# A recurrence decode that loads its next state block while it works, and weight casts issued three groups ahead

## The chip, the core and the metric

The kernel runs on one core of a Trainium2 chip. Its five engines work side by side, each through its own instruction queue in order: TensorE (PE; its weight loads are PEld), VectorE (DVE), ScalarE (ACT), GpSimd (POOL) and SyncE (SP), which issues all transfers here. The metric is the device time of one launch in microseconds (us).

## What is computed

One inference step of a two-layer decoder trunk. A prompt of 256 tokens and 8 decode tokens (one for each of 8 sequences) share all weights. Each layer has eight retention heads and sixteen heads of the RWKV-7 recurrence side by side, an output projection, and a gated feed-forward block of width 5632:

```python
xn   = rms_norm(h, g_attn);  proj = xn @ w_in            # 2048 -> 7456 columns
y_ret, s_ret = retention_mixer(proj[:, :4096], ret_state, ...)
y_rw,  s_rw  = rwkv7_mixer(shifted(proj[:, 4096:]), rwkv_state, ...)
h = h + concat(y_ret, y_rw) @ w_out
hn = rms_norm(h, g_ffn)
h = h + (silu(hn @ w_gate) * (hn @ w_up)) @ w_down

def step(s, inp):                      # the recurrence, for one token
    sa = einsum('bhvk,bhk->bhv', s, -kk)
    s  = s * w + sa[..., None] * (kk * a) + v[..., None] * k
    return s, einsum('bhvk,bhk->bhv', s, r)
```

For the 8 decode tokens the recurrence is one such step on a stored state of 128 x 64 x 64 numbers for each layer (8 sequences x 16 heads on the partitions).

## The kernel before, in words

**Weights.** All weights are packed into one stream of 128x128 blocks. `Stream` loads eight blocks at a time (`w_raw`, 512 KB, four buffers), rounds four at a time to fp32r on ACT (`w_hi`), and subtracts on DVE to get the rounding error (`w_lo`). Each block feeds three matmuls into the PSUM tile `st`: `w_hi` times the rounded activations, `w_hi` times their error, `w_lo` times the rounded activations. `proj` runs sixteen blocks for one output block; `contract` runs the blocks of the output projection and of `w_down`. The 19,872 `st` matmuls stand in a fixed order: per layer 59 projections for attention, the output projection in three phases (`W_OUT`: heads 0 to 3 of retention; recurrence pairs 0 to 3 with head 4; the rest), then the feed-forward block in four quarters.

**Side work.** Everything else is a set of generators. After every block `tick` lets each of them issue its next few instructions in the order of `RANK` (smaller first), by a small model of the engines' clocks, `Clock`; when PE has nothing to issue (`need`, `take`) only the side work goes on. So a fixed program comes out: each engine has its own order, and a matmul that needs a late tile holds up all matmuls behind it.

**The recurrence.** The sixteen heads go in eight pairs. `g_pair` prepares a pair; `g_levels` and `g_seq` (rank 2 and 1) run its chain over four chunks of 64 tokens: `py` on PE, its negative into `c_rT` (one half by DVE, one by ACT), then PE, ACT (`Z1`), PE, DVE (`r`), PE, ACT (`Z`), PE, DVE (`S`). Three buffers of the ring TM (8, shared with the tiles `h` of the residual stream) are held until a chain ends. `g_out` (rank 3) turns it into a block for the output projection.

**Its decode.** `g_rwkv_decode` (rank 4.5) starts when all pairs have given up their decode columns. It reads the state in eight blocks `dS` of 256 KB. For each block POOL multiplies it by one vector into `dT`, DVE sums that (`dec_sa`), DVE multiplies the block by another vector into a second `dT` and sums that (`dec_o`). `dS` and `dT` share two buffers (tag `d3`). At the end there is a norm, a transpose on PE (`o2`) and the tile `dec_y`, which POOL puts into the blocks of the output projection; phase 1 of `W_OUT` waits for it. `g_ret_state` (rank 5) does the like for the retention heads with `rkb`, `rS`, `rqb` in three buffers (tag `d2`); `g_update` (rank 6) writes the new recurrence state during the feed-forward block.

Of the kernel before, what the change touches and what calls it, by code (L numbers as in the profile page):

```python
# [19 lines left out]
P = 128  # L20
# [19 lines left out]
RC = 8  # L40
RAW_BUFS = 4
CH = 4
HL_BUFS = 4
CAP = {"st": 3, "pw": 5, "qa": 2, "qb": 2, "qc": 2, "gy": 3, "blk": 27, "TM": 8, "y": 1}
TA, RR, LV, UB, US, U2 = 4, 3, 2, 5, 5, 4
NORM_EPS = 1e-6
RET_EPS = 1e-5
RWKV_EPS = 64e-5
# [135 lines left out]


class Stream:
    def __init__(self, nc, clock, pools, src, ahead):
        self.nc, self.clock, self.pools, self.src = nc, clock, pools, src
        self.n = src.shape[0] * RC // CH
        self.raw, self.hi, self.lo = {}, {}, {}  # L190
        self.loaded = self.made = self.split = self.pos = 0
        self.ahead = ahead

    def load(self):
# [6 lines left out]
        r, i = divmod(c, RC // CH)  # L201
        return self.raw[r][:, i * CH:(i + 1) * CH]

    def make(self):
        r = self.made // (RC // CH)
        while self.loaded < min(self.src.shape[0], r + RAW_BUFS):
            self.load()
        h = self.hi[self.made] = self.pools[1].tile([P, CH, P], F32R, name="w_hi")
        self.nc.scalar.activation(out=h, in_=self.part(self.made), func=AF.Copy)
        self.made += 1  # L210

    def make_lo(self):
        c = self.split
        l = self.lo[c] = self.pools[2].tile([P, CH, P], F32R, name="w_lo")
        eng = self.nc.gpsimd if c < KB // CH else self.nc.vector
        eng.tensor_tensor(out=l, in0=self.part(c), in1=self.hi[c].bitcast(F32), op=ALU.subtract)
        self.split += 1

    def next(self):
        c, i = divmod(self.pos, CH)  # L220
        while self.made < min(self.n, c + 1 + self.ahead):
            self.make()
        while self.split < self.made and (self.split <= c + 1 or
                                          self.clock.at(self.hi[self.split]) <= self.clock.now + 100):
            self.make_lo()
        self.pos += 1
        return self.hi[c][:, i], self.lo[c][:, i]


EARLY = 150  # L230
GATE = 600
RANK = {"seq": 1, "levels": 2, "solve": 2, "pair": 3, "out": 3, "ret": 4, "rout": 4, "dec": 4.5, "state": 5, "upd": 6}


class Task:
# [7 lines left out]
class Kern:  # L243
# [4 lines left out]
    def __init__(self, ctx, tc, a, o):  # L248
        self.clock = Clock()
        self.tc, self.nc, self.a, self.o, self.ctx = tc, Core(tc.nc, self.clock), a, o, ctx  # L250
        nc = self.nc

        def pool(name, bufs=1, **kw):
            return Pool(ctx.enter_context(tc.tile_pool(name=name, bufs=bufs, **kw)), name, bufs, self.clock)

        self.const = pool("const")
        self.blk = pool("blk", bufs=CAP["blk"])
        self.st = pool("st", bufs=CAP["st"], space=PSUM)
        self.pw = pool("pw", space=PSUM)
# [7 lines left out]
        self.stream = Stream(nc, self.clock, (pool("w_raw", RAW_BUFS), pool("w_hi", HL_BUFS), pool("w_lo", HL_BUFS)), a["ws"],  # L267
                             HL_BUFS - 1)
# [455 lines left out]
    def g_seq(self, l, p, sv, AR, cf, LA, KA, TM, bv, Y):  # L724
# [6 lines left out]
        for c in range(NC):  # L731
# [5 lines left out]
                nc.tensor.matmul(py[:, 0:P], lhsT=ar, rhs=S, start=False, stop=True)  # L737
            yield 1
            rT = self.rT[:, c % 2]
            nc.vector.tensor_scalar(out=rT[lo, lo], in0=py[lo, lo], scalar1=-1.0, scalar2=None, op0=ALU.mult)  # L740
            nc.scalar.activation(out=rT[hi, hi], in_=py[lo, hi], func=AF.Copy, scale=-1.0)
            oc = un.tile([P, P], F32, name="oc", tag="us", bufs=US)
            nc.scalar.activation(out=oc[hi], in_=py[hi, 0:P], func=AF.Copy)
# [147 lines left out]
    def g_rwkv_decode(self, l, pds):  # L891
# [3 lines left out]
        scr = self.dr.tile([NS, NP, 2, 6, CW], F32, name="scr_dec")  # L895
        rows = 6 * NS
        for g in range(2):
            dt = de.tile([P, 4, P], F32, name="dec_t", tag="d3", bufs=2)
# [26 lines left out]
        od = de.tile([P, CW], F32, name="dec_o", bufs=1)  # L925
        sa = sm.tile([P, CW], F32, name="dec_sa", bufs=1)
        VB = 8
        for j in range(CW // VB):
            js = slice(j * VB, j * VB + VB)
            S = de.tile([P, VB, CW], F32, name="dS", tag="d3", bufs=2)  # L930
            nc.sync.dma_start(out=S, in_=self.a["s_rwkv"][l, :, js])
            yield 4
            for vec, dst in ((kr, sa), (wr, od)):
                tm = de.tile([P, VB, CW], F32, name="dT", tag="d3", bufs=2)
                eng = nc.gpsimd if vec is kr else nc.vector
                eng.tensor_tensor(out=tm, in0=S, in1=bc(vec, 1, VB), op=ALU.mult)
                yield 2
                nc.vector.tensor_reduce(out=dst[:, js], in_=tm, axis=AX.X, op=ALU.add)
                yield 4
        dd = sm.tile([P, 2], F32, name="dec_dd")  # L940
        for i, x in enumerate((kn, km)):
            t = sm.tile([P, CW], F32, name="dec_sq")
# [25 lines left out]
        for p in sorted(range(NP), key=lambda p: "b" not in self.Y[8 + p]):  # L968
# [3 lines left out]
            self.Y[8 + p]["dec"] = True  # L972
            yield 1

    def g_update(self, l):
        nc, de = self.nc, self.de
        w, v, km, sa, kn = self.upd
        VB = 8
        for j in range(CW // VB):
            js = slice(j * VB, j * VB + VB)  # L980
            S = de.tile([P, VB, CW], F32, name="uS", tag="d3", bufs=2)
            nc.sync.dma_start(out=S, in_=self.a["s_rwkv"][l, :, js])
            yield 13
# [71 lines left out]
    def g_ret_state(self, l, h, d, scr):  # L1055
# [270 lines left out]
    def layer(self, l):  # L1326
        nc = self.nc
        if l == 0:
# [301 lines left out]
```

## Time and profile before

| | us |
|---|---|
| median of 3 runs | 2911.83 (2911.44 to 2912.65) |
| the profiled execution | 2910.49 |
| its span, first to last instruction | 2908.6 |
| PE busy, weight loads busy | 2762.9 (95%), 2732.5 |
| DVE busy | 2047.8 (70%) |
| ACT busy | 1434.6 (49%) |
| POOL busy | 813.8 (28%) |

The profiled execution is 1.3 us below the median. 1.9 us of it lie outside the span. Layer 0 ends at about 1394 us; its attention and output projection take the time to about 692, and the feed-forward block the rest. The second layer has the same stages from 1394 to 2895.

### The profile page before, as it was taken

The page shows a single profiled execution, that of the slowest core. Times are in us where ns is not written, and L with a number is a line of the kernel's source. Part 1 is how long each engine was busy: PE and PEld are TensorE (multiplying, and loading weights), DVE is VectorE, ACT ScalarE, POOL GpSimd, SP SyncE. Part 2 cuts the span into 40 slices and gives each one's busy share as a digit, 9 for nine tenths or more (in the row PEclk, how much of TensorE's full clock was granted, in tenths as well). Part 3 has the DMA queues.
Part 4 walks back from the last instruction along what each step waited for, and adds up shares of the span by engine and source line. Part 5 has one row for each costly group of instructions (what it writes and reads, how often), then busy time and mean ns, then how long its engine had stood idle before and what let it go on. Part 6 is the DMA issues. An engine that isn't in the chain of part 4 may idle for free.

```text
span 2908.6 us, 58897 instructions
## 1 busy us (share of the span) xinstructions
PE 2762.9 (95%) x22304; PEld 2732.5 (94%) x22304; DVE 2047.8 (70%) x3964; ACT 1434.6 (49%) x2823; POOL 813.8 (28%) x1315
## 2 busy tenths in 40 slices
PE   7999999959999999999999999997899999999998
PEld 6998999859999999999999999996899999999998
DVE  7787777858856656666677778878688566665665
ACT  5554555425444444445555555543455454444454
POOL 4555655514500000000135655644153000000001
PEclk9999999979999999999999999998899999999999
DMA  5555555735655555555654545556466555555554
GB/s 171 158 161 162 157 161 165 234 111 191 223 182 181 181 182 181 182 181 182 204 171 131 169 154 181 166 171 212 146 201 209 181 181 182 182 181 182 181 182 138
DMA packets 230828, 512.46 MB, mean 176 GB/s; under 512 B 57488, under 2 KB 105872, under 8 KB 230544
## 3 DMA queue, kind: packets, MB, share of 16 engines
q1 hardware_dynamic: 230544, 508.70, 54.6%
q8 instruction: 175, 2.87, 0.4%
q14 instruction: 109, 0.89, 0.1%
HBM read 485.24 MB, written 23.38 MB: 175 GB/s over the span
## 4 chain that ended last, share of the span: by engine, by line
PE 81%; DVE 5%; DMA 2%; issue 1%; ACT 1%; POOL 1%; DVEq 0%; SPq 0%; POOLq 0%; ACTq 0%
PE st L161 73%; PE pw L161 7%; DVE w_lo L161 2%; DMA dS<-in_s_rwkv 1%; DVE on L161 1%; POOL dT L161 0%; DMA rkb<-scr_qk 0%; DVE dec_sa L161 0%; DVE dT L161 0%; DVE h L161 0%; ACT w_hi L161 0%; ACT rsw L161 0%; DVE blk L161 0%; DVE rS L161 0%; DVE q L161 0%
## 5 line engine op out<-in xcount | busy, mean ns | idle before, releaser
L161 PE MATMUL st<-blk,w_hi 128*128 128x264 f32 (+1 forms) x13248 | 2529.7, 290 | 27.0 <-DVE blk L161 19.4
L161 PEld LDWEIGHTS st<-blk,w_hi 128*128 128x128 f32 x13248 | 2064.4, 189 | 35.5 <-ACT w_hi L161 22.4
L161 PE MATMUL st<-blk,w_lo 128*128 128x264 f32 (+1 forms) x6624 | 1892.8, 286 | 13.1 <-DVE w_lo L161 10.2
L161 DVE TENSOR_TENSOR w_lo<-w_raw,w_hi 128x512 fp32r<-128x512 f32 x1652 | 1234.0, 752 | 595.0 <-ACT w_hi L161 564.4
L161 ACT ACTIVATE w_hi<-w_raw 128x512 fp32r<-128x512 f32 x1656 | 1043.2, 631 | 1162.4 <-PE st L161 1075.5
L161 PEld LDWEIGHTS st<-blk,w_lo 128*128 128x128 f32 x6624 | 1252.2, 189 | 17.1 <-DVE w_lo L161 12.7
L161 POOL TENSOR_TENSOR acc<-acc,sq 128x264 f32<-128x264 f32 x72 | 59.7, 829 | 1426.3 <-ACT sq L161 1425.9
L161 DVE TENSOR_TENSOR h<-h,st 128x264 f32<-128x264 f32 x224 | 94.8, 424 | 22.7 <-PE st L161 22.6
L161 POOL TENSOR_TENSOR sv_x<-sv_x,sv_t 32x15 f32<-32x15 f32 (+7 forms) x240 | 88.4, 368 | 18.8
L161 POOL TENSOR_TENSOR sv_t<-sv_m,sv_x 32x15 f32<-32x15 f32 (+7 forms) x240 | 84.1, 351 | 27.1 <-DMA sv_m<-scr_l 11.5
L161 ACT ACTIVATE c_rT<-pw 64x64 f32<-64x64 f32 x64 | 13.8, 216 | 89.1 <-DVE c_rT L161 88.8
L161 POOL TENSOR_TENSOR brs<-bve,c_nhalf 128x4 f32<-128x4 f32 (+3 forms) x42 | 41.5, 988 | 56.3 <-DVE bve L161 52.9
L161 ACT ACTIVATE Z<-pw 128x128 f32<-128x128 f32 x128 | 35.1, 274 | 41.8 <-PE pw L161 40.1
L161 POOL TENSOR_SCALAR mix_d<-mix_p,c_vec 128x8 f32<-128x8 f32 x54 | 34.7, 642 | 58.9 <-DVE mix_p L161 54.0
L161 POOL TENSOR_TENSOR Lm<-LA,c_m_lv 128x512 f32<-128x512 f32 x32 | 46.8, 1461 | 14.6 <-PE pw L161 14.5
L161 POOL TENSOR_TENSOR rqb<-rS,rqb 128x512 f32<-128x512 f32 x32 | 44.7, 1396 | 22.1 <-DMA rqb<-scr_qk 12.8
L161 POOL TENSOR_TENSOR uS<-uS,uT 128x512 f32<-128x512 f32 x32 | 48.6, 1519 | 2.5
L161 DVE TENSOR_TENSOR fg<-st,c_R 128x264 f32<-128x264 f32 x88 | 38.0, 432 | 13.7 <-PE st L161 13.0
L161 PE MATMUL pw<-c_ident,o 128*128 128x128 f32 x2 | 0.9, 447 | 48.6 <-DVE o L161 48.6
L161 DVE TENSOR_TENSOR fg<-st,fg 128x264 f32<-128x264 f32 x88 | 37.9, 431 | 12.2 <-PE st L161 12.2
L161 PEld LDWEIGHTS pw<-c_ident,o 128*128 128x128 f32 x2 | 0.4, 182 | 48.9 <-issue 48.9
L161 POOL TENSOR_TENSOR rkb<-rkb,v 128x512 f32<-128x512 f32 x32 | 35.2, 1099 | 39.4 <-DMA rkb<-scr_qk 39.4
(232 smaller groups left out, 2310.2 us busy)
## 6 DMA issues: line engine op xcount, KB each, us to landing
w_raw<-in_ws SPq DMA_DIRECT2D x828, 512.0 KB
rkb<-scr_qk SPq DMA_DIRECT2D x32, 256.0 KB
rS<-in_s_ret SPq DMA_DIRECT2D x32, 256.0 KB
rqb<-scr_qk SPq DMA_DIRECT2D x32, 256.0 KB
out_sts<-rS SPq DMA_DIRECT2D x32, 256.0 KB
h<-in_x SPq DMA_DIRECT2D x16, 264.0 KB
dS<-in_s_rwkv SPq DMA_DIRECT2D x16, 256.0 KB
uS<-in_s_rwkv SPq DMA_DIRECT2D x16, 256.0 KB
```

The costliest lines, as they stand in the source:

```text
L161: return f(*a, **kw)
```

## The change

Five things change.

1. In the decode of the recurrence `dec_load` issues the load of the next block right after POOL's product with the current one, and the second product of DVE goes into `dS` itself, so that a block has one `dT` and not two. The generator waits for the modelled end of a tile where it counted ticks before.
2. The tags `d2` (three buffers) and `d3` (two) become one ring `d` of five, used by the decode, the retention state and the state update. Rank of the decode: 4.5 to 1; of the retention state: 5 to 3.
3. `w_hi` has five buffers and not four, and is cast three groups ahead at a group's first block and four from the second; `w_lo` follows two or three groups ahead by position and no longer by the modelled end of `w_hi`. One `w_raw` tile fewer is loaded ahead, at the start too.
4. The first half of `c_rT` moves from DVE to ACT.
5. To make room, the rings `gy` (gates), `rr` and `u` lose a buffer each: 3 to 2, 3 to 2, 5 to 4.

```diff
-HL_BUFS = 4
-CAP = {"st": 3, "pw": 5, "qa": 2, "qb": 2, "qc": 2, "gy": 3, "blk": 27, "TM": 8, "y": 1}
-TA, RR, LV, UB, US, U2 = 4, 3, 2, 5, 5, 4
+HI_BUFS, LO_BUFS = 5, 4
+AHEAD = 3
+CAP = {"st": 3, "pw": 5, "qa": 2, "qb": 2, "qc": 2, "gy": 2, "blk": 27, "TM": 8, "y": 1}
+TA, RR, LV, UB, US, U2, DB = 4, 2, 2, 4, 5, 4, 5
...
-    def make(self):
-        r = self.made // (RC // CH)
-        while self.loaded < min(self.src.shape[0], r + RAW_BUFS):
-            self.load()
...
+    def make_hi(self, c):
+        while self.his <= min(c, self.n - 1):
+            r = self.his // (RC // CH)
+            while self.loaded < min(self.src.shape[0], r + RAW_BUFS - 1):
+                self.load()
+            h = self.hi[self.his] = self.pools[1].tile([P, CH, P], F32R, name="w_hi")
+            self.nc.scalar.activation(out=h, in_=self.part(self.his), func=AF.Copy)
+            self.his += 1
...
     def next(self):
         c, i = divmod(self.pos, CH)
-        while self.made < min(self.n, c + 1 + self.ahead):
-            self.make()
-        while self.split < self.made and (self.split <= c + 1 or
-                                          self.clock.at(self.hi[self.split]) <= self.clock.now + 100):
-            self.make_lo()
+        on = self.ahead > 0
+        self.make_hi(c + self.ahead + (on and i > 0))
+        self.make_lo(c + self.ahead - (on and i < 2))
...
-RANK = {"seq": 1, "levels": 2, "solve": 2, "pair": 3, "out": 3, "ret": 4, "rout": 4, "dec": 4.5, "state": 5, "upd": 6}
+RANK = {"seq": 1, "levels": 2, "solve": 2, "pair": 3, "out": 3, "ret": 4, "rout": 4, "dec": 1, "state": 3, "upd": 6}
...
-            nc.vector.tensor_scalar(out=rT[lo, lo], in0=py[lo, lo], scalar1=-1.0, scalar2=None, op0=ALU.mult)
+            nc.scalar.activation(out=rT[lo, lo], in_=py[lo, lo], func=AF.Copy, scale=-1.0)
...
+        S = self.dec_load(l, 0)
         for j in range(CW // VB):
             js = slice(j * VB, j * VB + VB)
-            S = de.tile([P, VB, CW], F32, name="dS", tag="d3", bufs=2)
-            nc.sync.dma_start(out=S, in_=self.a["s_rwkv"][l, :, js])
-            yield 4
-            for vec, dst in ((kr, sa), (wr, od)):
-                tm = de.tile([P, VB, CW], F32, name="dT", tag="d3", bufs=2)
-                eng = nc.gpsimd if vec is kr else nc.vector
-                eng.tensor_tensor(out=tm, in0=S, in1=bc(vec, 1, VB), op=ALU.mult)
-                yield 2
-                nc.vector.tensor_reduce(out=dst[:, js], in_=tm, axis=AX.X, op=ALU.add)
-                yield 4
+            yield (self.clock.at(S),)
+            tm = de.tile([P, VB, CW], F32, name="dT", tag="d", bufs=DB)
+            nc.gpsimd.tensor_tensor(out=tm, in0=S, in1=bc(kr, 1, VB), op=ALU.mult)
+            nxt = self.dec_load(l, j + 1) if j + 1 < CW // VB else None
+            yield (self.clock.at(tm),)
+            nc.vector.tensor_tensor(out=S, in0=S, in1=bc(wr, 1, VB), op=ALU.mult)
+            nc.vector.tensor_reduce(out=sa[:, js], in_=tm, axis=AX.X, op=ALU.add)
+            yield (self.clock.at(S),)
+            nc.vector.tensor_reduce(out=od[:, js], in_=S, axis=AX.X, op=ALU.add)
+            S = nxt
...
+    def dec_load(self, l, j):
+        S = self.de.tile([P, 8, CW], F32, name="dS", tag="d", bufs=DB)
+        self.nc.sync.dma_start(out=S, in_=self.a["s_rwkv"][l, :, 8 * j:8 * j + 8])
+        return S
```

What the change does to the order is seen at two places. The first is VectorE's queue in layer 0 where phase 0 of the output projection ends; `h` are its sums into the residual stream, `ret_y` the decode of the retention heads, `dec_sa` and `dec_o` the sums of the decode. Before:

```order
L161 TENSOR_SCALAR on<-pw,bmv,brs 16x128
L161 TENSOR_TENSOR h<-h,st 128x264
L161 TENSOR_TENSOR w_lo<-w_raw,w_hi 128x512
L161 TENSOR_REDUCE dec_sa<-dT 128x8
L161 TENSOR_TENSOR ret_y<-pw,rgd 128x16
L161 TENSOR_TENSOR ret_y<-ret_y,c_vec 128x16
L161 TENSOR_TENSOR h<-h,st 128x264
L161 TENSOR_TENSOR dT<-dS,dec_wr 128x512
L161 TENSOR_REDUCE dec_o<-dT 128x8
L161 TENSOR_REDUCE dec_sa<-dT 128x8
L161 TENSOR_TENSOR dT<-dS,dec_wr 128x512
```

After, VectorE's queue a little earlier in the same stretch; `r`, `S` and `o` belong to the last pair's chain, `ry` and `rS` to the retention heads:

```order
L162 TENSOR_TENSOR dS<-dS,dec_wr 128x512
L162 TENSOR_REDUCE dec_sa<-dT 128x8
L162 SCALAR_TENSOR_TENSOR ry<-pw,c_vec,rg 128x256
L162 TENSOR_REDUCE dec_o<-dS 128x8
L162 TENSOR_TENSOR r_8354<-c_rT,pw 128x128
L162 TENSOR_TENSOR dS<-dS,dec_wr 128x512
L162 TENSOR_REDUCE dec_sa<-dT 128x8
L162 SCALAR_TENSOR_TENSOR S<-pw,cf,Sc 128x128
L162 TENSOR_REDUCE dec_o<-dS 128x8
L162 TENSOR_TENSOR o<-pw,oc 64x128
L162 SCALAR_TENSOR_TENSOR rS<-rS,rkb 128x512
```

Before, the fourth of the eight blocks stands among the last sums `h` of phase 0, and four more follow with nothing between them; after, the fifth and sixth block shown here stand among the last chain's instructions, and the eighth is done before phase 0 ends. A block has three instructions on this queue both times.

The second place is SyncE's queue over the same stretch; `rkb`, `rS`, `rqb` and `out_sts` are the retention state's transfers. Before:

```order
L161 DMA w_raw<-in_ws 128x1024
L161 DMA h<-in_x 128x528
L161 DMA out_sts<-rS 128x512
L161 DMA w_raw<-in_ws 128x1024
L161 DMA dS<-in_s_rwkv 128x512
L161 DMA w_raw<-in_ws 128x1024 x2
L161 DMA dS<-in_s_rwkv 128x512 x4
L161 DMA w_raw<-in_ws 128x1024 x24
```

After:

```order
L162 DMA dS<-in_s_rwkv 128x512
L162 DMA out_sts<-rS 128x512
L162 DMA rkb<-scr_qk 128x4x128
L162 DMA dS<-in_s_rwkv 128x512
L162 DMA rS<-in_s_ret 128x512
L162 DMA dS<-in_s_rwkv 128x512
L162 DMA rqb<-scr_qk 128x4x128
L162 DMA dS<-in_s_rwkv 128x512
L162 DMA out_srp<-S 64x64 x2
L162 DMA h<-in_x 128x528
L162 DMA upg<-in_up 128x256
L162 DMA w_raw<-in_ws 128x1024
```

Before, the last four loads of `dS` follow each other behind the weights `w_raw`; after, the last four stand earlier, among the loads of the retention state, and none is left behind the weights.

## Rows read from the trace of the kernel before

**Rows 1.** Windows by stage: busy us of each engine, granted clock, DMA share, GB/s.
```profile
531.00:586.00 55.00, 47.81 (x346) 44.52 (x344) 49.54 (x120) 21.73 (x55) 26.11 (x30) 0.94 0.77 246
586.00:618.00 32.00, 1.52 (x7) 1.05 (x7) 15.08 (x36) 0.63 (x1) 7.98 (x14) 0.57 0.17 50
618.00:1394.00 776.00, 775.16 (x6373) 774.63 (x6373) 516.94 (x848) 378.90 (x650) 72.67 (x68) 1.00 0.57 185
...
1971.00:2018.00 47.00, 42.53 (x333) 40.56 (x331) 43.84 (x105) 20.07 (x47) 22.09 (x26) 1.00 0.80 259
2018.00:2046.00 28.00, 1.38 (x7) 0.64 (x5) 15.46 (x38) 0.63 (x1) 9.19 (x13) 0.55 0.17 56
2046.00:2895.00 849.00, 845.87 (x6948) 844.72 (x6948) 550.86 (x911) 419.95 (x725) 83.33 (x84) 1.00 0.56 181
```

**Rows 2.** Chain of waits, 586 to 618: start us, us, what.
```profile
588.40 2.89 DMA dS<-in_s_rwkv
...
591.42 1.27 POOL dT L161
592.71 0.70 DVE dec_sa L161
...
594.22 2.75 DMA dS<-in_s_rwkv
...
611.03 0.69 DVE dec_o L161
...
617.32 0.87 PE st L161 x2
```

**Rows 3.** Waits of VectorE, 586 to 618: us in total, times, longest.
```profile
DVE dec_sa L161 <- POOL dT L161: 14.1, 4, 3.7
```

**Rows 4.** Waits of VectorE, 2018 to 2046.
```profile
DVE dec_sa L161 <- POOL dT L161: 9.9, 4, 3.7
```

**Rows 5.** Waits of TensorE, whole span.
```profile
PE pw L161 <- DVE o L161: 48.6, 2, 28.8
...
PE pw L161 <- ACT c_rT L161: 12.2, 9, 2.8
PE st L161 <- DVE w_lo L161: 10.2, 7, 3.8
```

**Rows 6.** Tile c_rT, whole span: idle time of its engines, us and times.
```profile
  DVE c_rT L161: 88.8, 53
```

**Rows 7.** Tile c_rT, 531 to 618: duration ns min/median/max, first and last start.
```profile
L161 DVE TENSOR_SCALAR c_rT<-pw x4: 206/208/209, 534.1 to 561.6; 64x64 f32<-64x64 f32 x4
```

**Rows 8.** Groups of VectorE, 531 to 586: busy us, mean ns, idle before.
```profile
L161 DVE TENSOR_TENSOR w_lo<-w_raw,w_hi 128x512 fp32r<-128x512 f32 x21 | 17.7, 854 | 0.4 <-ACT w_hi L161 0.4
```

**Rows 9.** Groups of VectorE, 700 to 1390.
```profile
L161 DVE TENSOR_TENSOR w_lo<-w_raw,w_hi 128x512 fp32r<-128x512 f32 x474 | 347.3, 736 | 218.6 <-ACT w_hi L161 208.3
```

**Rows 10.** Timeline of VectorE, 706 to 730: start us, us, instruction.
```profile
709.50 0.43 DVE L161 TENSOR_TENSOR fg<-st,c_R 128x264 f32<-128x264 f32 x1 [0.18 <-PE st L161]
...
710.95 1.27 DVE L161 SCALAR_TENSOR_TENSOR fg<-fth,fg 128x264 f32<-128x264 f32 x1
...
718.28 0.42 DVE L161 TENSOR_TENSOR blk<-fg,blk 128x264 fp32r<-128x264 f32 x1
...
721.30 0.43 DVE L161 TENSOR_TENSOR fg<-st,c_R 128x264 f32<-128x264 f32 x1 [0.18 <-PE st L161]
...
722.45 0.42 DVE L161 SCALAR_TENSOR_TENSOR fg<-fth,fg 128x264 f32<-128x264 f32 x1
```

**Rows 11.** Windows of the st matmuls alone, after the first gap.
```profile
617.30:620.00 2.70, 2.68 (x12) 2.68 (x13) 0.00 (x0) 0.00 (x0) 0.50 0.64 191
620.00:622.00 2.00, 2.00 (x13) 2.00 (x13) 0.35 (x1) 0.00 (x0) 0.68 0.01 4
...
700.00:702.00 2.00, 2.00 (x18) 2.00 (x18) 0.00 (x0) 0.00 (x0) 1.00 0.59 219
```

**Rows 12.** Waits of SyncE's queue, 531 to 618.
```profile
SPq L161 <- DVE dT L161: 13.7, 4, 5.3
```

More of the change, by code (lines that the diff above doesn't have):

```diff
@@ L186, with __init__ @@
 class Stream:
-    def __init__(self, nc, clock, pools, src, ahead):
-        self.nc, self.clock, self.pools, self.src = nc, clock, pools, src
+    def __init__(self, nc, pools, src, ahead):
+        self.nc, self.pools, self.src = nc, pools, src
         self.n = src.shape[0] * RC // CH
         self.raw, self.hi, self.lo = {}, {}, {}
-        self.loaded = self.made = self.split = self.pos = 0
+        self.loaded = self.his = self.los = self.pos = 0
         self.ahead = ahead
@@ L202, in part, with make_lo @@
         return self.raw[r][:, i * CH:(i + 1) * CH]
-    def make(self):
-        r = self.made // (RC // CH)
-        while self.loaded < min(self.src.shape[0], r + RAW_BUFS):
-            self.load()
[L208 to L217, printed above, removed]
+    def make_hi(self, c):
[6 more added lines that the diff above has]
+            self.his += 1
+    def make_lo(self, c):
+        while self.los <= min(c, self.n - 1):
+            l = self.lo[self.los] = self.pools[2].tile([P, CH, P], F32R, name="w_lo")
+            eng = self.nc.gpsimd if self.los < KB // CH else self.nc.vector
+            eng.tensor_tensor(out=l, in0=self.part(self.los), in1=self.hi[self.los].bitcast(F32), op=ALU.subtract)
+            self.los += 1
     def next(self):
         c, i = divmod(self.pos, CH)
-        while self.made < min(self.n, c + 1 + self.ahead):
-            self.make()
-        while self.split < self.made and (self.split <= c + 1 or
-                                          self.clock.at(self.hi[self.split]) <= self.clock.now + 100):
-            self.make_lo()
+        on = self.ahead > 0
+        self.make_hi(c + self.ahead + (on and i > 0))
+        self.make_lo(c + self.ahead - (on and i < 2))
         self.pos += 1
@@ L266, in __init__ @@
         self.dr = pool("dr", bufs=2, space=DRAM)
-        self.stream = Stream(nc, self.clock, (pool("w_raw", RAW_BUFS), pool("w_hi", HL_BUFS), pool("w_lo", HL_BUFS)), a["ws"],
-                             HL_BUFS - 1)
+        self.stream = Stream(nc, (pool("w_raw", RAW_BUFS), pool("w_hi", HI_BUFS), pool("w_lo", LO_BUFS)), a["ws"],
+                             AHEAD)
         self.tasks, self.pos, self.used, self.last = [], 0, dict.fromkeys(CAP, 0), {}
@@ L897, in g_rwkv_decode @@
         for g in range(2):
-            dt = de.tile([P, 4, P], F32, name="dec_t", tag="d3", bufs=2)
+            dt = de.tile([P, 4, P], F32, name="dec_t", tag="d", bufs=DB)
             ps = yield from self.pget()
@@ L980, in g_update @@
             js = slice(j * VB, j * VB + VB)
-            S = de.tile([P, VB, CW], F32, name="uS", tag="d3", bufs=2)
+            S = de.tile([P, VB, CW], F32, name="uS", tag="d", bufs=DB)
             nc.sync.dma_start(out=S, in_=self.a["s_rwkv"][l, :, js])
@@ L986, in g_update @@
             for x, y in ((v, km), (sa, kn)):
-                t = de.tile([P, VB, CW], F32, name="uT", tag="d3", bufs=2)
+                t = de.tile([P, VB, CW], F32, name="uT", tag="d", bufs=DB)
                 nc.gpsimd.tensor_tensor(out=t, in0=bc(x[:, js], 2, CW), in1=bc(y, 1, VB), op=ALU.mult)
@@ L1060, in load @@
         def load(j, n):
-            t = de.tile([P, 4, P], F32, name=n, tag="d2", bufs=3)
+            t = de.tile([P, 4, P], F32, name=n, tag="d", bufs=DB)
             if n == "rS":
@@ L1335, in layer @@
                     nc.sync.dma_start(out=self.hp[k // 2], in_=self.a["x"][k // 2])
-                    if k % 4 == 0 and k < 4 * RAW_BUFS:
+                    if k % 4 == 0 and k < 12:
                         self.stream.load()
@@ L1354, in layer @@
             lora.append(self.spawn(self.g_lora(l, j, self.proj(TP)), 1, "mix"))
-            self.stream.ahead = HL_BUFS - 1
+            self.stream.ahead = AHEAD
         self.Y = [{} for _ in range(16)]
```

## The prediction

> **What bounds the kernel now.** I read the windows by stage first. In the feed-forward stretches TensorE is busy in 775.2 of 776 us and in 845.9 of 849 us, at the full granted clock [rows 1]. Nothing in the side work can shorten those stretches; they can only be made longer. What is left lies in attention and in the output projection. There two windows stand out: from 586 to 618 us TensorE is busy 1.5 of 32 us, from 2018 to 2046 us 1.4 of 28 us [rows 1]. The list of TensorE's waits puts nearly all of that down to one wait in each layer, 48.6 us in two [rows 5]; it ends when the decode of the recurrence hands over.
>
> The chain of waits shows what is done there. A block of the decode is a load of 2.6 to 2.9 us, POOL's product of 1.27 us, and DVE's sum and product of 0.70 us each; only then is its buffer free and the next load starts, 5.8 us after the one before [rows 2]. So DVE waits 14.1 us in four waits in layer 0 [rows 3] and 9.9 us in four in layer 1 [rows 4], with TensorE waiting behind it. From the last `dec_o` at 611.03 to the first matmul at 617.32 there are 6.3 us of norm and transpose [rows 2].
>
> Just ahead of these windows it is DVE that is short: 49.5 of 55 us busy from 531 to 586, 43.8 of 47 us from 1971 to 2018 [rows 1]. That limits what the change can bring: TensorE doesn't wait for the decode alone, but for all DVE work that stands ahead of it.
>
> **The decode, layer 0.** By the order shown, a block has three DVE instructions before and after. The product is written into `dS` and not into a second tile, which changes no work. So I keep DVE's work from 531 us to the end of the gap, 49.5 + 15.1 = 64.6 us [rows 1], and take away only idle time. With the next `dS` under way while POOL works, DVE's waits for `dT` go: 14.1 us [rows 3]. The blocks move forward into a stretch where DVE has other work, so their own waits for load and POOL are covered by it; without that cover a block would cost at least POOL's 1.27 us ahead of DVE. What stays idle is about 21.7 - 14.1 = 7.6 us, from 86.3 us of time less 64.6 us of work: 5.5 us were idle before 586, and the end of the decode (the norm's `pow` on POOL, the transpose, the put) has small waits still. SP issues eight loads of `dS` as before, in another place.
>
> **A price for it.** The four `dT` of POOL that ran beside an idle DVE now run beside a busy one. In the feed-forward stage `w_lo` takes 736 ns on average, in the stretch from 531 to 586, with POOL busy 26.1 of 55 us, 854 ns [rows 8, 9]; that is 118 ns more at POOL busy 47%, so some 0.25 us for one DVE product that meets a POOL product. With two such meetings for each `dT` I charge 0.5 us, 2.0 us for four. A single meeting can cost more: the product `fg` took 1.27 us once and 0.42 us the next time [rows 10]. The Trainium skill (SBUF — State Buffer, section "SBUF: two separate sides") says that a DVE instruction with two SBUF inputs and a POOL instruction share a port pair that the first holds for its whole length, the other being fully blocked; this trace agrees in kind, by the same 1.27 us. By that rule, taken at its worst, each of the four would hold DVE for a whole product, and the charge would be 5.1 us. I take 2.0 and keep 4 x 1.27 = 5.1 us, from the duration of `dT` [rows 2], for the range.
>
> **The half of `c_rT` on ACT.** Four `c_rT` of 0.21 us leave DVE in this stretch [rows 7]: 0.8 us. Layer 0 in sum: 14.1 + 0.8 - 2.0 = 12.9 us.
>
> **The decode, layer 1.** The same with 9.9 us [rows 4], 0.4 us for two `c_rT` (an estimate, half of layer 0's), and 2.0 us again for POOL: 9.9 + 0.4 - 2.0 = 8.3 us.
>
> **The clock behind the gap.** After the gap TensorE's clock is granted at 0.50, the 1.2 GHz level, for 2.7 us and at 0.68 for 2 us: 25 matmuls in 4.7 us, where the full clock runs 9 in 1 us [rows 11]. 25 / 9 = 2.8 us, so 1.9 us are lost in each layer. A wait remains ahead of the same matmul, only shorter, so I take half of it back: 2 us for both layers.
>
> **Waits elsewhere in attention.** ACT waits 88.8 us in 53 times for DVE's half of `c_rT` [rows 6], and TensorE waits 12.2 us in 9 times for the tile [rows 5]. With both halves on ACT the detour over DVE's queue is gone; ACT gets 0.2 us more for each and can itself be late with a weight cast ahead of it. I count 5 of the 12.2 us. TensorE waits 10.2 us in 7 times for a `w_lo` [rows 5], each time because DVE was held up longer than the casts run ahead. `w_hi` now comes up to a group earlier (twelve matmuls, 12 / 9 = 1.3 us at the rate of rows 11) and `w_lo` a part of that; I count 3 of 10.2 us. Together 8 us; the bounds are nothing gained and 6 us lost to new waits of this kind, and 22.4 us.
>
> **What I cost at nothing.** In the feed-forward stages casts come earlier, but DVE's waits there are for `w_hi` (208 of 218.6 us idle before `w_lo` [rows 9]) while TensorE never waits, so nothing is gained. The ring `gy` of two: one `fg` lives from 709.50 to 718.70 and the next is written at 721.30 [rows 10], so no more than one is alive and the third buffer covered nothing. If that were wrong, each of the 88 gate groups would pay. `rr` and `u` hold short-lived tiles; their risk is in the 6 us above. At the start one `w_raw` fewer is loaded ahead, while TensorE waits for the first activations anyway. The merged ring adds SP waits; SP waited for `dT` 13.7 us in four times already, at most 5.3 us [rows 12], while weights are loaded several groups ahead.
>
> **The sum.** 12.9 + 8.3 + 2 + 8 = 31.2 us. The profiled execution of 2910.5 us would become 2879.3; the median of the runs is 1.3 us above it, 2880.6, so I predict 2880 us.
>
> **Rivals.**
> *The gap closes further.* If DVE's remaining idle time of these stretches went too (18 us in layer 0, and in layer 1, by 47 + 28 - 43.8 - 15.5 = 15.7 us idle, some 15 us), the clock were back at once (4 us) and all 22.4 us of the small waits went, it would be 59 us: 2853 us. Against it: the chain from `dec_o` to the first matmul stays, and DVE stays the short engine.
>
> *Only part of it.* With the charge of 5.1 us for POOL in each layer, no clock gained and 6 us lost elsewhere, 9.8 + 5.2 - 6 = 9 us remain: 2903 us.
>
> *The wait moves to the last chain, no change.* The decode now ranks with the chain and stands between its `r` and `S` on DVE. A chain passes DVE with `r` and `S` in each of four chunks; if each pass waits for a whole block, 3 x 0.69 us, that is 8 x 2.1 = 17 us a layer, 33 us in all, and it eats the gain: about 2911 us. For it: the residual tiles of phase 0 need TM buffers that the last chain holds, so TensorE stops until that chain is through. Against it: this is work that DVE has to do in any case before the gap's end; it costs only where DVE then idles.
>
> *Weights come late, slower.* `dS`, `dT` and the retention tiles take their five buffers in turn, and SP issues in order. A load of `dS` whose buffer is not free holds up every `w_raw` behind it. The longest such hold now is 5.3 us [rows 12]. The casts are three groups ahead and a loaded tile is two groups more, 5 x 1.3 = 6.5 us of matmuls; a hold beyond that stops TensorE one for one. With sixteen loads it takes 2.4 us beyond the cover for each, holds of 9 us and not 5.3, to use up the gain and 6 us more: 2918 us. Below holds of 6.5 us it costs nothing.
>
> **How the numbers follow.** A difference of 0.2%, 5.8 us, is about what a measurement of this kernel can tell from none. I give the forecast (2863 to 2897 us) 0.60, the further gain (below 2863) 0.12, the part gain (2897 to 2906) 0.13, no change 0.08, slower 0.07. The range from 2855 to 2903 us leaves out the two last and the ends of the part and the further gain, some 2 in 10. Faster by over 0.2%: 0.85; within: 0.08; slower: 0.07.
>
> **What would show it.** In the profile after: the window with almost no matmul in each layer shrinks from 32 and 28 us to under 15; the chain of waits no longer has `DMA dS` in it; DVE's waits for `dT` under 4 us; DVE busy over 85% up to the end of the gap; `w_lo` slower than 854 ns there; TensorE's waits for `c_rT` under 7 us. The feed-forward windows should be the same to 1 us. The prediction would be wrong if TensorE waits longer for the last chain in phase 0 than it gains at its end, if waits for `w_raw` show up on ACT, or if anything moves in the feed-forward stage.

## The result, and the profile after

The changed kernel takes 2860.1 us (median of 4 runs, 2856.8 to 2867.4), the kernel before, beside it, 2912.2 (4 runs, 2911.4 to 2914.9): a ratio of 0.9823, 95% interval [0.9802, 0.9844]. It is 52 us faster; 32 us were forecast (2880), and the range of 2855 to 2903 holds it. The profiled execution takes 2861.97 us, 48.5 less than that of before, with a span of 2860.2.

The windows by stage of the changed kernel answer to [rows 1]; the stages lie earlier here.

```profile
522.00:588.00 66.00, 52.40 (x343) 47.82 (x341) 61.44 (x144) 23.19 (x60) 31.80 (x33) 0.84 0.61 198
588.00:591.00 3.00, 0.30 (x1) 0.14 (x1) 2.25 (x9) 0.12 (x1) 1.70 (x6) 0.77 0.29 113
591.00:1372.00 781.00, 778.46 (x6359) 776.99 (x6360) 507.54 (x846) 376.28 (x648) 73.92 (x71) 0.99 0.56 184
...
1937.00:1992.00 55.00, 45.25 (x334) 42.52 (x333) 54.11 (x125) 19.56 (x45) 29.02 (x31) 0.97 0.77 245
1992.00:1996.00 4.00, 0.87 (x5) 0.44 (x3) 3.75 (x12) 1.00 (x3) 1.69 (x5) 0.99 0.51 159
1996.00:2846.00 850.00, 846.04 (x6943) 843.98 (x6943) 548.29 (x919) 417.01 (x726) 88.72 (x89) 1.00 0.56 181
```

The two windows almost without matmuls are down from 32 and 28 us to 3 and 4. DVE, which idled for half of them, is now busy 61.4 of 66 and 54.1 of 55 us ahead of them. TensorE's waits over the whole span (us in total, times, longest) answer to [rows 5]:

```profile
PE st L162 <- DVE blk L162: 18.2, 5, 15.8
PE st L162 <- DVE w_lo L162: 10.2, 10, 2.3
PE st L162 <- DVE h L162: 9.9, 8, 2.5
PE pw L162 <- DVE r L162: 6.2, 6, 1.5
...
PE pw L162 <- ACT Z L162: 4.6, 7, 1.2
...
PE pw L162 <- DVE o L162: 2.5, 3, 1.4
...
PE pw L162 <- ACT c_rT L162: 0.5, 1, 0.5
```

The wait for `o` fell from 48.6 us to 2.5 and that for `c_rT` from 12.2 to 0.5. The wait for `w_lo` is 10.2 us as before, and that for `h` is up from 3.3 to 9.9 us, all of it in the stretches around the end of the decode (3.2 and 6.7). DVE's own waits from 522 to 592 us, against [rows 3]; from 1937 to 1996, against [rows 4], it shows a single one of 0.3 us:

```profile
DVE h L162 <- DMA h<-in_x: 1.3, 1, 1.3
DVE dS L162 <- POOL dT L162: 1.1, 1, 1.1
DVE o L162 <- PE pw L162: 0.9, 1, 0.9
DVE dec_y L162 <- PE pw L162: 0.5, 1, 0.5
DVE r L162 <- PE pw L162: 0.4, 1, 0.4
```

The chain of waits of layer 0 from 558 to 592 us (start us, us, what), against [rows 2]:

```profile
557.97 2.90 DMA dS<-in_s_rwkv
561.04 1.26 POOL dT L162
562.33 1.20 DVE dS L162
...
568.48 1.69 DVE dS L162
...
579.76 0.60 DVE dec_o L162
...
581.95 0.68 DVE w_lo L162
582.63 0.34 DVE h L162
582.98 0.60 DVE w_lo L162
583.58 0.34 DVE h L162
...
588.93 0.32 PE pw L162
...
590.38 0.60 POOL blk L162
591.02 1.09 PE st L162 x3
```

Before, four loads of `dS` stood in the chain and the last `dec_o` was followed by 6.3 us of norm and transpose alone. Now one load is left in it, and the last `dec_o` comes 11 us ahead of the end: the norm runs among `w_lo` and `h`, which DVE has to do anyway. This is a chain of DVE's own work. In layer 1 no load of `dS` is left in the chain between 1937 and 1996 us, but one of weights, `w_raw`, of 5.1 us (from 1974.96).

**Where the 48.5 us lie.** The 19,872 matmuls into `st` stand in the same order in every kernel here, so that the n-th is the same work. I divide each layer at three of them: attention from number 0 (9440 in layer 1) to 2785 (12700), and the *closing stretch* with the last chain and the gap from there to 3024 (12960). Number 9440 is not the first of layer 1: that is 9936, and the 496 before it are the end of layer 0's feed-forward block, which goes on to 1463 us in the kernel before and does not end at 1394. These 496 take 61 us in every kernel here, so the differences stand. Two limits of these figures: the side work is not tied to the `st` matmuls and can move from one stretch to the next, and each kernel's stretches come from one execution, while four runs of the changed kernel lie 10.6 us apart. Before, the closing stretches are 531.5 to 617.3 and 1971.2 to 2045.8 us; after, 522.2 to 591.0 and 1937.3 to 1995.6:

```profile
522.20:591.00 68.80, 52.51 (x342) 47.76 (x341) 63.49 (x151) 23.31 (x60) 33.50 (x38) 0.84 0.60 194
1937.30:1995.60 58.30, 45.42 (x333) 42.36 (x331) 57.19 (x134) 20.27 (x48) 30.08 (x33) 0.97 0.76 241
```

The closing stretches are 85.8 - 68.8 = 17.0 and 74.6 - 58.3 = 16.3 us shorter. Attention ahead of them is 514.4 - 506.4 = 8.0 and 569.3 - 556.9 = 12.4 us shorter. The start (first `st` matmul at 15.8 and not 17.1 us) gives 1.3; the rest of the layers takes 4.9 and 1.8 us more. Together 48.3.

### The profile page after: what moved, and what is told of

The parts are those of the page before. It is cut to its first block, busy times and chain, and to the rows that moved or that the text cites. A ratio compares the mean times of both kernels' runs of the same rounds, so it can differ in the third digit from the quotient of the medians.

```text
span 2860.2 us, 59139 instructions
## 1 busy us (share of the span) xinstructions
PE 2765.1 (97%) x22298; PEld 2736.1 (96%) x22298; DVE 2025.0 (71%) x3900; ACT 1438.6 (50%) x2887; POOL 830.3 (29%) x1316
## 4 chain that ended last, share of the span: by engine, by line
PE 78%; DVE 8%; POOL 3%; DMA 3%; issue 2%; ACT 0%; SPq 0%; DVEq 0%; POOLq 0%; ACTq 0%
PE st L162 71%; PE pw L162 7%; DVE w_lo L162 3%; DMA w_raw<-in_ws 1%; POOL uS L162 1%; DMA uS<-in_s_rwkv 1%; POOL sv_x L162 1%; POOL sv_t L162 1%; POOL uT L162 0%; DVE on L162 0%; DVE h L162 0%; DVE bdb L162 0%; DVE rS L162 0%; DVE dS L162 0%; DVE blk L162 0%
## 5 line engine op out<-in xcount | busy, mean ns | idle before, releaser
L162 PE MATMUL st<-blk,w_lo 128*128 128x264 f32 (+1 forms) x6624 | 1891.8, 286 | 12.1 <-DVE w_lo L162 10.2
L162 DVE TENSOR_TENSOR w_lo<-w_raw,w_hi 128x512 fp32r<-128x512 f32 x1652 | 1256.2, 766 | 459.5 <-PE st L162 372.6
L162 PEld LDWEIGHTS st<-blk,w_lo 128*128 128x128 f32 x6624 | 1253.8, 189 | 15.7 <-DVE w_lo L162 12.9
L162 POOL TENSOR_TENSOR sv_x<-sv_x,sv_t 32x15 f32<-32x15 f32 (+7 forms) x240 | 91.9, 383 | 18.8
L162 DVE TENSOR_TENSOR blk<-fg,blk 128x264 fp32r<-128x264 f32 x88 | 46.2, 525 | 14.0 <-ACT blk L162 14.0
L162 ACT ACTIVATE c_rT<-pw 64x64 f32<-64x64 f32 x128 | 27.6, 215 | 52.2 <-PE pw L162 51.1
L162 POOL TENSOR_TENSOR brs<-bve,c_nhalf 128x4 f32<-128x4 f32 (+3 forms) x42 | 44.0, 1050 | 30.6 <-DVE bve L162 30.1
L162 ACT ACTIVATE fth<-fg 128x264 f32<-128x264 f32 x88 | 37.3, 424 | 24.6 <-DVE fg L162 24.6
L162 POOL TENSOR_TENSOR uS<-uS,uT 128x512 f32<-128x512 f32 x32 | 48.6, 1519 | 2.4
L162 ACT ACTIVATE blk<-h,c_vec 128x264 fp32r<-128x264 f32 x64 | 32.0, 513 | 34.3 <-DVE h L162 28.5
```

The lines of the kernel that those rows point to most:

```text
L162: return f(*a, **kw)
```

## The experiments

The first theory was that the new decode alone empties the closing stretches; its rivals gave the gain to the casts, to ranks or to the accident of the order. Each expectation below names its own theories A and B. The table has all kernels, divided at the same matmuls: D, C and R are decode, casts (with the smaller rings) and `c_rT`; "idle" is TensorE's idle time in both attentions, window less busy time. The column "us" has the median of each kernel's runs, and "to before" its distance to the kernel before in the same comparison; the other columns are from its profiled execution.

| kernel | us | to before | both attentions | idle there | closing stretches |
|---|---|---|---|---|---|
| before | 2910 to 2912 | | 1083.7 | 43.4 | 85.8 + 74.6 |
| D | 2882.2 | -30.1 | 1081.7 | 46.3 | 71.2 + 60.9 |
| C | 2892.9 | -19.3 | 1056.1 | 29.5 | 81.2 + 83.8 |
| R | 2886.5 | -25.8 | 1066.6 | 30.4 | 80.3 + 67.8 |
| D and C | 2881.4 | -30.6 | 1082.7 | 43.3 | 67.4 + 59.4 |
| D and R | 2891.3 | -20.7 | 1082.1 | 44.8 | 65.7 + 70.4 |
| C and R | 2880.6 | -29.6 | 1061.8 | 29.3 | 82.0 + 64.2 |
| all three (the changed kernel) | 2860.1 | -52.1 | 1063.3 | 31.2 | 68.8 + 58.3 |
| before, 61 ns | 2912.0 | +1.6 | 1078.3 | 43.1 | 85.4 + 74.1 |
| before, 140 ns | 2914.9 | +4.5 | 1081.0 | 42.6 | 90.6 + 73.3 |
| changed, 61 ns | 2872.8 | -39.5 | 1069.0 | 35.4 | 69.8 + 61.2 |
| changed, old ranks | 2869.2 | -41.3 | 1068.8 | 36.0 | 66.9 + 60.4 |
| changed, no early load | 2865.1 | -45.3 | 1061.2 | 30.7 | 67.1 + 64.3 |
| before, one ring of five | 2893.5 | -18.4 | 1078.9 | 42.5 | 78.6 + 64.9 |

**The decode alone (D).** The kernel before with the new loop, the ring and the ranks:

```
-TA, RR, LV, UB, US, U2 = 4, 3, 2, 5, 5, 4
+TA, RR, LV, UB, US, U2, DB = 4, 3, 2, 5, 5, 4, 5
-... "dec": 4.5, "state": 5, ...
+... "dec": 1, "state": 3, ...
+        S = self.dec_load(l, 0)
...
+            nxt = self.dec_load(l, j + 1) if j + 1 < CW // VB else None
```

> The kernel before with the decode alone changed: next dS loaded while the block works, one ring d of five, ranks dec 1 and state 3. Casts, c_rT and the other rings as before. Theory A (all idle time of DVE around the end of the decode goes, by the new decode alone): the two stretches give 17 + 16 = 33 us as they did in the changed kernel, less 1 us for c_rT that stays on DVE: 2880 us, windows almost without matmul under 8 us. Theory B (the extra gain over my forecast comes from the casts that run ahead and fill DVE): only the forecast's 12 + 8 = 20 us, 2892 us, windows of 12 to 20 us remain.

2882.2 us, ratio 0.9909 [0.9887, 0.9930]; stretches 14.6 and 13.7 us shorter. Theory A, to 2 us in the time: the decode alone gives 28.3 of the 33.3 us that the closing stretches lose in the changed kernel, and the casts aren't needed for that. Attention is 7.0 us shorter in layer 0 and 5.0 longer in layer 1.

**The casts alone (C).** The kernel before with the new `Stream`, five `w_hi`, three loads at the start, and the smaller rings `gy`, `rr` and `u`.

```
-        while self.made < min(self.n, c + 1 + self.ahead):
-            self.make()
...
+        self.make_hi(c + self.ahead + (on and i > 0))
+        self.make_lo(c + self.ahead - (on and i < 2))
```

> The kernel before with the new issue order of the casts and its rings (w_hi 5, w_lo 4, gy 2, rr 2, u 4, three w_raw loads ahead of the x loads); decode and c_rT as before. Theory A (the casts gain nothing in attention, since TensorE's waits for w_lo stayed 10.2 us in the changed kernel, and cost the 4 to 6 us lost in the feed-forward of layer 0): 2913 to 2918 us, less 1 us at the start. Theory B (the casts ahead give the gain in attention away from the decode): 2912 - 10 = 2902 us or less.

2892.9 us, ratio 0.9942 [0.9923, 0.9961]. Attention is 27.6 us shorter, the closing stretch of layer 1 is 9.2 longer; there all eight blocks of the decode lie in it now, before it was seven. Theory A falls, and B is exceeded. The smaller rings were not run apart from the casts.

**`c_rT` alone (R).** One line of the kernel before:

```
-            nc.vector.tensor_scalar(out=rT[lo, lo], in0=py[lo, lo], scalar1=-1.0, ...)
+            nc.scalar.activation(out=rT[lo, lo], in_=py[lo, lo], func=AF.Copy, scale=-1.0)
```

> The kernel before with the one line of c_rT moved to ACT. Theory A (TensorE's 12.2 us of waits for c_rT are real and go): 2900 to 2903 us, TensorE's waits for c_rT under 3 us. Theory B (the waits move to the next late operand, h or r): 2909 to 2915 us, with as much more wait for others as is gone from c_rT.

2886.5 us, ratio 0.9915 [0.9901, 0.9930]: twice what A gave it. `c_rT` is gone from TensorE's waits; these rows of that list show what is left and what came:

```profile
PE pw L161 <- DVE o L161: 39.3, 2, 25.5
...
PE pw L161 <- DVE ryd L161: 10.7, 3, 7.4
PE pw L161 <- DVE r L161: 9.3, 11, 2.1
```

Part of the wait moved to `r` and `ryd`, as B said, and still 17.1 us went in attention and 12.3 in the closing stretches, where the four and two halves of 0.21 us make 1.2 us of DVE's work. But DVE's busy time in these stretches fell by more, from 64.1 to 59.1 and from 59.1 to 55.2 us, and its idle time only from 21.7 to 21.2 and from 15.5 to 12.7: most of the 12.3 us is other DVE work that lies ahead of the stretches here, in layer 1 one block of the decode among it.

**The changed kernel, planned with another latency.** `Clock.LAT` is a number that the planner assumes; no work changes, only the order in places.

```
-    LAT = 60
+    LAT = 61
```

> The changed kernel with only the planner's assumed latency at 61 ns in place of 60, which shifts the order of issue in places and changes no work. Theory A (the gain is that of the three edits): 2857 to 2864 us, within 4 us of the changed kernel. Theory B (gains and losses of up to 9 us per 400 matmuls in attention are accidents of the order): more than 6 us away from it, either side.

2872.8 us, ratio 0.9869 [0.9854, 0.9884]: 12.7 us more than the changed kernel. Theory B: the order of issue alone is worth that much here. So the next kernels were read by stretches.

**The kernel before, planned otherwise, twice.** `LAT = 61`, and `EARLY = 140` in place of 150.

> The kernel before with only the planner's assumed latency at 61 ns in place of 60; no work changes. Theory A (the order of issue alone moves the time by some 10 us either way, as the same edit moved the changed kernel by 12.7 us): 2895 to 2925 us, the two stretches at the end of the decode (last chain and gap, 85.8 and 74.7 us) within 8 us of their times. Theory B (the kernel before is an unlucky order, and any change of it would have gained): under 2895 us.

> The kernel before with only the planner's look-ahead at 140 in place of 150 ns; no work changes. A second draw of the same kind. Theory A: 2895 to 2925 us. Theory B: under 2895 us.

2912.0 us (ratio 1.0007 [0.9997, 1.0016]) and 2914.9 us (1.0017 [1.0008, 1.0027]). Theory A both times. Two other orders of the kernel before gain nothing, so it is not shown to be an unlucky one, and the gains of D, C and R (30, 19 and 26 us) are beyond this and beyond the 12.7 us of the changed kernel.

**The changed kernel with the old ranks.**

```
-... "dec": 1, "state": 3, ...
+... "dec": 4.5, "state": 5, ...
```

> The changed kernel with the old ranks, dec 4.5 and state 5. Told by the two stretches from the last chain to the end of the gap (68.8 and 58.3 us in the changed kernel, 85.8 and 74.7 us before), since the whole time moves by some 10 us with the order alone. Theory A (what counts is that loads no longer stand in the chain; the ranks only choose who goes first on a DVE that is busy anyway): both stretches within 4 us of the changed kernel's, 2855 to 2875 us. Theory B (it is the rank that brings the blocks forward into a stretch with other DVE work; without it each of the four late blocks waits for POOL, 4 x 1.27 = 5 us a layer at the least): stretches 5 to 10 us longer each, 2870 to 2885 us.

2869.2 us, ratio 0.9861 [0.9846, 0.9875]; stretches 66.9 and 60.4 us, within 2.1 of the changed kernel's. Theory A: the ranks don't carry it.

**The changed kernel without the early load.**

```
-        S = self.dec_load(l, 0)
         for j in range(CW // VB):
...
+            S = self.dec_load(l, j)
             yield (self.clock.at(S),)
...
-            nxt = self.dec_load(l, j + 1) if j + 1 < CW // VB else None
```

> The changed kernel with each dS loaded at the start of its own block instead of one block earlier; ring, ranks and products as in the changed kernel. Told by the same two stretches (68.8 and 58.3 us). Theory A (the early loads take the waits out): each block waits for its load of 2.6 to 2.9 us and POOL's 1.27 us again, as far as DVE has nothing else; four late blocks a layer give 8 to 15 us each, 2876 to 2890 us. Theory B (the rank alone does it, since the blocks then lie where DVE has other work): within 4 us each, 2855 to 2875 us.

2865.1 us, ratio 0.9849 [0.9834, 0.9863], an interval that overlaps that of the changed kernel. Layer 0 does as well without it (67.1 us), layer 1 loses 6.0. Mostly B: the early load, like the ranks, can be left out of layer 1 for a few us and of layer 0 for nothing. Either the two stand in for each other, or something else that both kernels keep does the main part.

**The kernel before with one ring of five.** That candidate is the ring: with free buffers SP issues the next `dS` by itself.

```
-            S = de.tile([P, VB, CW], F32, name="dS", tag="d3", bufs=2)
+            S = de.tile([P, VB, CW], F32, name="dS", tag="d", bufs=DB)
```

(and so for all tiles of `d3` and `d2`)

> The kernel before with the two rings of the decode, update and retention tiles (two and three buffers) merged into one of five; loads in the code at the start of their block, ranks 4.5 and 5, casts and c_rT as before. Told by the stretches from the last chain to the end of the gap (85.8 and 74.7 us before; 68.8 and 58.3 us in the changed kernel; without the early load 67.1 and 64.4, with the old ranks 66.9 and 60.4). Theory A (the free buffers are what takes the waits out: SP runs ahead by itself, so that neither the early load in the code nor the rank was needed): stretches 10 to 17 us shorter each, 2880 to 2892 us. Theory B (the early load and the rank replace each other, and with neither the old waits stay): within 4 us of before in each, 2905 to 2916 us.

2893.5 us, ratio 0.9931 [0.9915, 0.9948]: between the two. DVE's wait for `dT` from 527 to 606 us:

```profile
DVE dec_sa L161 <- POOL dT L161: 4.7, 3, 2.2
```

It was 14.1 us [rows 3]; in layer 1 it falls from 9.9 [rows 4] to 1.5. So the ring alone takes out 17.8 of the 24.0 us of waits and gives 7.2 + 9.7 = 16.9 of the 28.3 us that D gives in the closing stretches. The rest comes from what D has beside the ring: the early load, the rank, the product written in place (so that a block takes two buffers and not three) and the generator's waiting by modelled ends. These were not parted further.

**The changed kernel without one of its parts.** The old issue of the casts (D and R, the small rings kept), `c_rT` on DVE (D and C), and the old decode (C and R):

> The changed kernel with the old issue order of the casts (four w_hi, four w_lo, four w_raw loads ahead at the start); decode, c_rT and small rings as changed. Theory A (the gains in attention overlap: casts alone gave 9.7 + 18.0 us and c_rT alone 7.7 + 9.5 us there, but both with the decode only 8.0 + 12.4 us, so either one suffices): within 10 us of the changed kernel, 2855 to 2872 us. Theory B (they add up): the 19.8 us of casts alone are lost, 2878 to 2884 us.

2891.3 us, ratio 0.9928 [0.9913, 0.9943]. Beyond even theory B: attention is 18.8 us longer than in the changed kernel and the closing stretch of layer 1 is 12.1 us longer.

> The changed kernel with its half of c_rT back on DVE. Theory A (overlap, as above): 2855 to 2872 us, TensorE's waits for c_rT back at 5 us or more, others less. Theory B (they add up): 25.8 us are lost, 2884 to 2890 us.

2881.4 us, ratio 0.9895 [0.9880, 0.9910]. Nearly B. TensorE waits 9.8 us for `c_rT` again:

```profile
PE pw L162 <- ACT c_rT L162: 9.8, 8, 3.0
```

> The changed kernel with the decode as it was before (loads at the start of a block, two dT, rings d3 of two and d2 of three, ranks 4.5 and 5); casts, c_rT and the small rings as changed. Told by TensorE's stretches. Theory A (the decode is worth in the changed kernel what its two stretches show, 17.0 + 16.4 us, and casts and c_rT give the rest in attention ahead of them, 8.0 + 12.4 us): 2890 to 2897 us, the two gaps with 25 us or more without matmuls again, attention ahead of them 15 to 25 us shorter than before. Theory B (casts and c_rT together give 20 + 26 us as they do alone, and the decode only the rest): 2863 to 2872 us.

2880.6 us, ratio 0.9896 [0.9880, 0.9913], between the two. The closing stretches are 13.2 and 5.9 us longer than in the changed kernel, less than the 17.0 and 16.3 by which that one beats the kernel before. The old waits are back in the closing stretch of layer 0 (DVE's waits, 516 to 598 us):

```profile
DVE dec_sa L162 <- POOL dT L162: 12.2, 4, 4.0
```

With the seven kernels of the table each part has four prices. Decode: -30.1 alone, -11.3 with the casts, +5.1 with `c_rT`, -22.5 with both. Casts: -19.3, -0.5, -3.8, -31.4 (alone, with D, with R, with both). `c_rT`: -25.8, +9.4, -10.3, -21.5 (alone, with D, with C, with both). Their means are 14.7, 13.8 and 12.1 us. The ratios are known to 4 to 6 us either way, so -0.5, -3.8 and +5.1 can't be told from nothing. None of the twelve kernels is faster than the changed one.

## Why the prediction was right, and too small

**What bounded the kernel** was read rightly: the two windows almost without matmuls went (3 and 4 us; under 15 were forecast), and `dT` holds DVE for 1.1 us (under 4). That "the chain of waits no longer has `DMA dS` in it" is wrong by one load of 2.90 us in layer 0, which stands ahead of the gap.

**The decode: 12.9 and 8.3 us forecast, 17.0 and 16.3 measured.** The mechanism was right: DVE's idle time went. Its size has two parts. In the closing stretches DVE's idle time fell from 85.8 - 64.1 = 21.7 to 5.3 us and from 74.6 - 59.1 = 15.5 to 1.1: by 16.4 and 14.4, where I took the waits for `dT` alone, 14.1 and 9.9. The step that failed is "What stays idle is about 21.7 - 14.1 = 7.6 us", with "the norm's `pow` on POOL, the transpose, the put" that "has small waits still". Those were idle only because the decode was the last thing that DVE had; once it ends 11 us ahead of the end, they lie among `w_lo` and `h`. That is 2.3 and 4.5 us of the miss. The other 1.8 and 3.5 are DVE's work, which I let grow by 1.2 and 1.6 us and which fell by 0.6 and 1.9 (64.1 to 63.5, 59.1 to 57.2). In layer 1 part of it lies ahead of the stretch now: seven decode products and fourteen sums stood in it before, five and twelve now. Of the rivals, *the gap closes further* (2853 us) came nearest, by its first condition. (Its 18 us for layer 0 have no working; the prediction's own figures make the idle time there 21.7.) *The wait moves to the last chain* came in small at most: over the whole span TensorE waits 13.0 us for `r`, `Z` and `S`, before 8.6, and 6.6 us more than before for `h`.

**The price, 2.0 us a layer.** I expected `w_lo` slower than 854 ns. The groups of DVE in the closing stretch of layer 0 (busy us, mean ns, idle before):

```profile
L162 DVE TENSOR_TENSOR w_lo<-w_raw,w_hi 128x512 fp32r<-128x512 f32 x22 | 16.0, 727 | 0.0
L162 DVE TENSOR_TENSOR dS<-dS,dec_wr 128x512 f32<-128x512 f32 x8 | 7.9, 987 | 1.2 <-POOL dT L162 1.1
...
L162 DVE TENSOR_REDUCE dec_sa<-dT 128x8 f32<-128x512 f32 x8 | 5.4, 673 | 0.0
...
L162 DVE SCALAR_TENSOR_TENSOR rS<-rS,rkb 128x512 f32<-128x512 f32 x4 | 4.5, 1137 | 0.0
```

In the kernel before the same groups, with the same counts, have means of 846, 685, 682 and 718 ns. So the product pays 8 x 0.30 = 2.4 us and `rS` 4 x 0.42 = 1.7, while `w_lo` gets 22 x 0.12 = 2.6 back: 1.5 net of 4.1 gross. The size was about right; what paid was not what I had named.

**`c_rT` in the closing stretches: 0.8 and 0.4 us forecast.** Alone (R) it gave 5.5 and 6.8 us there, but mostly because other DVE work had moved ahead. Beside the new decode it gives nothing that can be told: 67.4 and 59.4 us with a half on DVE, 68.8 and 58.3 with both on ACT. So these runs don't speak against the small forecast. What I counted was the busy time that leaves DVE. ACT's half also waited for DVE's half, 88.8 us in 53 times [rows 6], and a late one can delay `r`, `Z` and `S` behind it; that this is what gave R its 17.1 us in attention is likely but not shown, since the order of issue changed with it.

**The clock, 2 us:** not gained in layer 0, and some 1 us in layer 1 (an estimate from the windows). The windows behind its gap (granted clock third from the end), against [rows 11]:

```profile
591.00:593.00 2.00, 1.98 (x8) 1.98 (x9) 0.00 (x0) 0.00 (x0) 1.62 (x10) 0.50 0.53 152
593.00:595.00 2.00, 2.00 (x11) 2.00 (x11) 0.78 (x2) 0.63 (x1) 0.93 (x6) 0.50 0.28 111
595.00:597.00 2.00, 2.00 (x13) 2.00 (x13) 0.58 (x2) 0.40 (x1) 0.00 (x0) 0.64 0.01 4
```

The 1.2 GHz level is still granted for 4 us and more after a gap of 3 us instead of 32. In layer 1 the clock is 0.57 from 1995.6 to 1999.6 us and full behind that; before it was 0.50 from 2046 to 2050 and 0.63 for 2 us more.

**Waits elsewhere: 8 us forecast, 20.4 measured in attention.** This is the largest miss, and its step is "I count 5 of the 12.2 us" and "I count 3 of 10.2 us". TensorE's waits for `c_rT` fell by 11.7 us and not 5, those for `w_lo` by nothing and not 3. `c_rT` alone gives 17.1 us there and the casts alone 27.6. The reason that I gave for the casts isn't shown: `w_lo` holds TensorE for 10.2 us in the changed kernel too. Of TensorE's idle time in attention 12.2 us went (43.4 to 31.2). The other 8.2 are in its busy time, of which the two kernels of before with another plan also show 5.1 and 1.9; the granted clock is 0.99 on average there before and after and explains little of them.

**The feed-forward "the same to 1 us"** was wrong in the letter: behind the closing stretches layer 0 takes 4.9 us more and layer 1 1.8. The two kernels of before with another plan show 2.9 and 3.2 more in layer 0, 0.3 and 2.1 in layer 1; so some 2 us a layer may be the change's. About 2.4 us of layer 0's (an estimate) are TensorE's clock: it is granted at 0.50 from 591.0 to 596.4 us and at 0.51 from 674.9 to 678.4, the second time after 4 us with TensorE busy for 2.4, and before at 0.50 from 617.3 to 621.3 alone. TensorE's waits for `w_lo` there are 0.8 us in each layer. No cost of the rings `gy`, `rr` and `u` can be seen.

**Weights late** cost nothing that can be seen: TensorE waits 1.4 us for `w_hi` in the whole span, before 0.7, and SP's longest hold for a decode tile in the closing stretches is 6.1 us, under the cover of 6.5 that I had worked out. But the sign that I named for it, waits of ACT for `w_raw`, did come: 42.6 us in 19 waits, where before it was one of 33.3 and six that make 8.6.

**What was luck.** The mechanism of the decode was right. That the range holds the time is in part luck: my terms missed by 12.1 us (decode), 12.4 (attention) and 1.3 (start) one way and by 8.7 (clock and feed-forward) the other. The time lies 5 us inside the end of the range, and the order of issue alone is worth as much.

**What stays open.** Casts or `c_rT` alone bring attention down to some 30 us of idle time, and together no further (29.3). With the new decode either one alone gives nothing there (43.3 and 44.8), both give it again (31.2). In layer 0 all eight blocks lie behind this stretch in these kernels, so there it isn't their work on DVE. The merged ring also feeds the retention state, and the order changes everywhere; which of them does it was not settled. Nor was how much of the changed kernel's 52 us is a fortunate order: three near relatives (no early load, other ranks, other latency) stand 5.0, 9.1 and 12.7 us above it, the first of them within the noise.

## What to carry to other kernels

When a serial tail is taken out of a chain on a busy engine, count all of that engine's idle time up to the tail's end, not only the waits that the edit names: what still waits then lies beside other work. The busy time of an instruction in a chain over two engines is not its price, and neither is its gain alone a price beside other edits: 0.21 us on DVE in 64 places, 13.4 us in all, gave 25.8 us alone, 21.5 as the last of three edits and a loss of 9.4 beside the new decode. And where a planner fixes the order, plan the same work with another constant once or twice before a gain of ten microseconds is put down to an edit. Look for the free buffer first: a ring of five, with the loads where they were in the code, gave 16.9 of the 28.3 us in the closing stretches.

## What the runs showed of the hardware

DVE's product `dS`, with two SBUF inputs, takes up to 1.77 us beside a product of POOL, where its least is 0.67; the reductions of the decode, with one input of the same size, stay between 0.66 and 0.68. One such meeting in the timelines of DVE and of POOL (start us, us, instruction):

```profile
567.80 0.69 DVE L162 TENSOR_TENSOR w_lo<-w_raw,w_hi 128x512 fp32r<-128x512 f32 x1
568.40 1.77 DVE L162 TENSOR_TENSOR dS<-dS,dec_wr 128x512 f32<-128x512 f32 x1
570.09 0.67 DVE L162 TENSOR_REDUCE dec_sa<-dT 128x8 f32<-128x512 f32 x1
```

```profile
567.81 1.82 POOL L162 TENSOR_TENSOR rqb<-rS,rqb 128x512 f32<-128x512 f32 x1 [1.46 <-DVE bmv L162]
```

POOL's product (1.26 us at its shortest) is longer by 0.56, nearly what `w_lo` takes, and `dS` ends 0.54 us after it, a little less than its own shortest length. The Trainium skill (SBUF — State Buffer, section "SBUF: two separate sides") says that such instructions hold a shared port pair for their whole length and that the other side blocks fully; these rows agree with it. By that rule I had put the worst case at 5.1 us a layer; the two groups that pay took 4.1 more than before in layer 0.

By another row, a meeting can cost more than one product of POOL. The longest `w_lo` of the changed kernel takes 4.26 us; it is the second of the two in this row of DVE, beside four instructions of POOL in a row:

```profile
262.40 4.90 DVE L162 TENSOR_TENSOR w_lo<-w_raw,w_hi 128x512 fp32r<-128x512 f32 x2
```

```profile
262.54 0.98 POOL L162 TENSOR_TENSOR brs<-bve,c_nhalf 16x1 f32<-16x1 f32 x1
263.49 1.30 POOL L162 TENSOR_TENSOR Lm<-LA,c_m_lv 128x512 f32<-128x512 f32 x1
264.76 1.28 POOL L162 TENSOR_TENSOR XT<-sv_c,c_m_b 128x512 f32<-128x512 f32 x1
266.00 0.74 POOL L162 TENSOR_TENSOR km<-km,mix_k 128x264 f32<-128x264 f32 x1
```

So four meetings at one POOL product each, 5.1 us, is not the most that they could cost; the longest product `dS` here took 1.77 us.
